# Value tiles of their own, third-chunk operands over finished gate sums, and S5 rows kept as loaded, in one layer of a streaming encoder on one Trainium2 core

## The chip, the cores and the metric

The kernel runs on one core of a Trainium2 chip. The metric is the device time of one execution in microseconds (us), as the median of several runs. An engine is named as in the profile: PE (TensorE matrix passes) and PEld (its weight loads), DVE (VectorE), ACT (ScalarE), POOL (GpSimd) and SP (SyncE, which in this kernel issues the loads and stores). Each engine works through its own instructions in order; semaphores tie the engines together.

## The reference

The reference computes one step of an encoder layer for two groups of requests with shared weights: one prompt of 1024 tokens and 8 decode requests of 16 tokens. The kernel treats them as 1152 tokens of width 1024.

```
h = rmsnorm(x, g_pre1);  z = h @ w_in
u_ssm, u_pool, q_mem = z[:, :512], z[:, 512:768], z[:, 768:]
y_ssm = gelu(s5_scan(u_ssm))
y_ssm = y_ssm * sigmoid(y_ssm @ w_glu + b_glu)
y_pool = multiscale_pool(u_pool);  y_mem = attention(q_mem, mem_k, mem_v)   # decode: cached k, v
gates = sigmoid(h @ w_gate + b_gate)            # 3 x 1024 columns
merged = gates_0 * (y_ssm @ w_br_ssm) + gates_1 * (y_pool @ w_br_pool) + gates_2 * (y_mem @ w_br_mem)
x += rmsnorm(merged @ w_out, g_post1)
x += rmsnorm(conv_ffn(rmsnorm(x, g_pre2)), g_post2)
```

All data are float32, and the outputs include the new states.

## The kernel before

**Precision and passes.** A matrix product in the kernel is three passes over operands that are split in two. `split` (L60 to L63) makes the split of a tile: ACT copies a rounded high part (L62), DVE subtracts it from the tile (L63, the low part). `mm3` (L100 to L106) issues high by high (L102), high by low (L105) and low by high (L106). Names that end in hi and lo are such pairs; a weight is loaded into a tile `rawt` (`load_raw`, L67) and split into `whi` and `wlo`.

**Tokens.** The 1152 tokens lie in three chunks of 384. A matrix pass is 128 x 384, and a result tile of 128 x 384 takes one bank of PSUM. There are two groups of four banks, called pc and ps in the profile.

**Order.** One scheduler goes through the whole program and lists the instructions of each engine in the order in which they seem ready to it; calls like `high_priority`, `keep_in_program_order` and `issue_after` steer it. A tile taken from a pool waits until the last use of the buffer that it gets. Nearly all loads and stores are issued by SP, in order, so a load that waits for its buffer holds up all loads and stores behind it.

**Stages that matter here.**

- *Phase 1.* Projection, S5 scan, pooling branch and attention. Attention of the decode requests (`attention_decode`, L719) is interleaved with that of the prompt. For its second half, four value tiles `cv` of 512 KB are loaded (L765), each for two requests, and multiplied with the transposed probabilities `PT` (L768, 16 small matrix instructions a tile). All four take tag "U", a pool of two buffers. The prompt's attention issues L847 to L850 (scores), L851 (exponential on ACT), L854 (values), L855 and L856 (division on DVE).
- *Gates in phase 1.* Interleaved with this, gate columns 8 to 15 for all chunks, then (L925 on) the gates that are needed for chunk 2, odd ones first. Their sigmoids are kept in memory (`Dsg`).
- *`blocks`* (L953). The remaining 16 gate columns of chunks 0 and 1 are computed by Strassen's method. For this, x of chunks 0 and 1 is loaded again (tiles `xT`, L164, behind the last `cv` load by `issue_after`), scaled by the norm (L962) and combined into operand blocks B11, B21 and others, tiles `bB` and `bT`, each split into a high and a low part. The first products with B11 and B21 stand in the gate loop of phase 1: the product with B11 is copied into a tile `u` (L942), eight of which (tag "su") live until phase S.
- *Phase S* (`phase_s`, L986). For eight pairs of gate columns j, five block products each, which are added to `u` (L1054 to L1062, partly on POOL), passed through a sigmoid (L1047) and stored in `Dsg` (L1048). At pair 6 the operands of the branches for chunks 0 and 1 are loaded (`load_pair`, L1091: attention results from `Dmem`, pooling results from `Dpool`) and split into `ohi` and `olo`.
- *Phase G* (`phase_g`, L1139). Branch weights `w_bmp` are loaded, then the operands of chunk 2 (the call of `operands`, the line behind the first `load_w`). For each column tile f and chunk c the two branches MEM and POOL are multiplied, weighted by the gate tiles `sgl` (L1085) and added to `merged`. Then GLU (`glu`, L1115) for each chunk: `load_ssm` loads the S5 output rows (L1101) into `br` tiles and splits them; the product with `w_glu` goes through a sigmoid on ACT (L1122); POOL adds the two halves of the S5 row together again as `ys` (L1124); DVE multiplies (L1125); and the result is split for the last branch (`w_brs`).

The next stages (phase O and the feed-forward network) stay as they are. The rows `rb` hold the norm's factors of a chunk, spread over the partitions.

Of the kernel before, what the change touches and what calls it, by code (L numbers as in the profile page):

```python
# [7 lines left out]
F32 = mybir.dt.float32  # L8
# [23 lines left out]
class K:  # L32
# [685 lines left out]
    def attention_decode(self, P):  # L718

        nc = self.nc  # L720
        cq = P.tile([128, 768], F32, tag="CA", name="cq")
        Qbd = cq[:, 0:512].rearrange("p (h b e s) -> p h b e s", h=2, b=8, e=2)
        nc.gpsimd.memset(cq[:, 0:512], 0.0)
        qdt = cq[:, 512:768].rearrange("p (h j k) -> p h j k", h=2, j=8)
        for hp in range(2):
            nc.sync.dma_start(qdt[:, hp], self.Dq[hp].rearrange("p (j k) -> p j k", j=8)[:, :, 128:144])
        for hp in range(2):
            qd = qdt[:, hp].rearrange("p j (b k) -> p b j k", k=2)
            for e in range(2):
                es = slice(64 * e, 64 * e + 64)  # L730
                nc.gpsimd.tensor_copy(Qbd[es, hp, :, e, :].rearrange("p b (j k) -> p b j k", k=2), qd[es])
        sc = [self.sm().rearrange("p (h m) -> p h m", h=2) for _ in range(2)]
        for b in range(8):
            if b % 2 == 0:
                ck = P.tile([128, 2, 2, 256], F32, tag="U", name="ck")
                nc.sync.dma_start(ck, self.I["ck"][b // 2])
            r = 32 * (b % 4)
            for hp in range(2):
                nc.tensor.matmul(sc[b // 4][r:r + 32, hp, :], Qbd[:, hp, b].rearrange("p e s -> p (e s)"),
                                 ck[:, b % 2, hp, :], start=True, stop=True, tile_position=(0, r))  # L740
        yield
        mx = P.tile([128, 4], F32, tag="mxd", name="mx")
        for e in range(2):
            nc.vector.tensor_reduce(mx[:, 2 * e:2 * e + 2], sc[e], axis=AX.X, op=OP.max)
        nc.vector.tensor_scalar(mx, mx, -0.125, None, op0=OP.mult)
        rs = P.tile([128, 4], F32, tag="rsum", name="rsum")
        p = P.tile([128, 4, 256], F32, tag="bc", name="pd")
        for h in range(4):
            nc.scalar.activation(p[:, h, :], sc[h // 2][:, h % 2, :], AF.Exp, bias=mx[:, h:h + 1], scale=0.125,
                                 accum_out=rs[:, h:h + 1])  # L750
        nc.vector.reciprocal(rs, rs)
        nc.vector.tensor_mul(p, p, rs[:, :, None].to_broadcast([128, 4, 256]))
        PT = P.tile([128, 4, 2, 128], F32, tag="V", name="PT")
        for a in range(2):
            t = self.sm().rearrange("p (h m l) -> p h m l", h=2, m=2)
            for h in range(2):
                for m in range(2):
                    nc.tensor.transpose(t[:, h, m, :], p[:, 2 * a + h, m * 128:(m + 1) * 128], self.ident)
            nc.vector.tensor_copy(PT[:, 2 * a:2 * a + 2], t)
        yield  # L760
        od = self.sm().rearrange("p (b h s) -> p b h s", b=8, h=2)
        for b in range(8):
            if b % 2 == 0:
                cv = P.tile([128, 2, 2, 256], F32, tag="U", name="cv")
                self.att_half = nc.sync.dma_start(cv, self.I["cv"][b // 2])  # L765
            for hp in range(2):
                for m in range(2):
                    nc.tensor.matmul(od[:, b, hp, :], cv[:, b % 2, m, hp * 128:hp * 128 + 128],  # L768
                                     PT[:, 2 * (b // 4) + hp, m, 32 * (b % 4):32 * (b % 4) + 32], start=m == 0, stop=m == 1)
        ot = P.tile([128, 2, 8, 16], F32, tag="tmp", name="otd")  # L770
        for hp in range(2):
            for e in range(2):
                es = slice(64 * e, 64 * e + 64)
                nc.vector.tensor_copy(ot[es, hp].rearrange("p j (b k) -> p b j k", k=2),
                                      od[es, :, hp, 16 * e:16 * e + 16].rearrange("p b (j k) -> p b j k", k=2))
        for hp in range(2):
            nc.sync.dma_start(self.Dmem[hp].rearrange("p (j k) -> p j k", j=8)[:, :, 128:144], ot[:, hp])
        yield
# [84 lines left out]
    def phase1(self):  # L863
        nc, tc = self.nc, self.tc
# [7 lines left out]
        self.Dsg = D.tile([24, 3, 128, 384], F32, name="Dsg")  # L872
        self.rbs = ExitStack()
        self.rb = self.rbs.enter_context(tc.tile_pool(name="rb", bufs=1)).tile([128, 3, 384], F32, name="rb")
        su = self.rbs.enter_context(tc.tile_pool(name="su", bufs=8))
        with ExitStack() as ctx:
            def pool(name, bufs):
                return ctx.enter_context(tc.tile_pool(name=name, bufs=bufs))
# [55 lines left out]
            self.su = []  # L934
            for m in self.strassen_gates()[0::2]:
                gw = gates(m, (2,))
                self.su.append(su.tile([128, 384], F32, tag="su", name="u"))
                for n, ks in (("B11", slice(0, 4)), ("B21", slice(4, 8))):
                    b = self.block(self.pc(), [w[:, ks] for w in gw], n)
                    with tc.high_priority():  # L940
                        if n == "B11":
                            nc.scalar.activation(self.su[-1], b, AF.Copy)  # L942
                        else:
                            sg = P.tile([128, 384], F32, tag="sg", name="sg")
                            nc.vector.tensor_add(sg, self.su[-1], b)
                            nc.scalar.activation(sg, sg, AF.Sigmoid, bias=self.vec[:, V_BGATE + m:V_BGATE + m + 1])
                            nc.sync.dma_start(self.Dsg[m, 0], sg)
# [44 lines left out]
    def phase_s(self):  # L992
        nc, tc = self.nc, self.tc
        V, G = nc.vector, nc.gpsimd
        with ExitStack() as ctx:
            def pool(name, bufs):
# [4 lines left out]
            P = self.P = _Multi(None, {n: self.gs.enter_context(tc.tile_pool(name="g" + n, bufs=b, side="right",  # L1001
                                                                             reuse_waits="tile"))
                                       for n, b in (("pl", 5), ("opa", 16))})
            self.om, self.op = [], []

            def operands(c, tag):
# [62 lines left out]
            for j in range(8):  # L1069
                cur, nxt = nxt, weights(j + 1) if j < 7 else None  # L1070
                if j == 6:
                    for c in range(2):
                        operands(c, "opa")
                for p in (6, 5, 7, 3, 4):
                    prod(cur, p)

# [16 lines left out]

    def load_ssm(self, P, c):

        op = []
        for q in range(0, 4, 2):
            r = self.rawtile([128, 2, 384], "br")
            for j, n, k0, k1, col in self.pieces(c):
                for i in range(n):  # L1100
                    self.nc.sync.dma_start(r[:, :, col + 144 * i:col + 144 * i + k1 - k0],  # L1101
                                           self.DY[q:q + 2, 7 - j - i, :, :, k0:k1].rearrange("q c g k -> (c g) q k"))
            op += [self.split_op(P, r[:, i], "opb") for i in range(2)]
        return op

    def split_op(self, P, r, tag):
        t = [P.tile([128, 384], F32R, tag=tag, name=n) for n in ("ohi", "olo")]
# [6 lines left out]

    def glu(self, P, w, c):  # L1115
        nc = self.nc
        y = self.load_ssm(P, c)
        out = []
        for o in range(4):
            b = self.proj(w[o // 2], c, 4, lambda kt, c: y[kt][0], lambda kt, c: y[kt][1], wk=4 * (o % 2))  # L1120
            sg = P.tile([128, 384], F32, tag="sg", name="sg")
            nc.scalar.activation(sg, b, AF.Sigmoid, bias=self.vec[:, V_BGLU + o:V_BGLU + o + 1])  # L1122
            ys = P.tile([128, 384], F32, tag="pl", name="ys")
            nc.gpsimd.tensor_add(ys, y[o][0].bitcast(F32), y[o][1].bitcast(F32))  # L1124
            nc.vector.tensor_mul(sg, ys, sg)  # L1125
            out.append(self.split_op(P, sg, "opa" if c < 2 else "opb"))
        return out

    def branch(self, P, bw, nk, wk, g, f, c, x):
# [9 lines left out]
    def phase_g(self):  # L1139
        nc, tc = self.nc, self.tc  # L1140
        with ExitStack() as ctx:
            def pool(name, bufs):
                return ctx.enter_context(tc.tile_pool(name=name, bufs=bufs, side="right", reuse_waits="tile"))
            P = self.P
            P.by.update({"opb": pool("gopb", 22), "sg": pool("gsg", 4)})
            bw = self.load_w(self.I["w_bmp"][0])
            self.operands(2, "opb")
            om, op = self.opx(self.om), self.opx(self.op)
            self.merged = [self.mtile([128, 8, 384], F32, f"mg{c}") for c in range(3)]
            for f in range(8):  # L1150
# [682 lines left out]
def emit(tc, I, O, dbg=None, stop=99):  # L1833
    with ExitStack() as ctx:
        k = K(tc, ctx, I, O, dbg)
        k.consts()
        k.phase1()
        if stop < 2:
            return
        k.phase_s()  # L1840
        k.rbs.close()
        k.phase_g()
        k.gs.close()
        k.dump("merged", k.merged[0])
        if stop < 3:
            return
        with tc.tile_pool(name="w2", bufs=4, reuse_waits="tile") as w2:
            k.w2 = w2
            k.phase_o()
            k.phase_u()  # L1850
            k.phase_d()
# [142 lines left out]
```

## Time and profile before

| | us |
|---|---|
| median of 3 runs | 1559.93 (1559.21 to 1562.07) |
| profiled execution | 1558.77 |
| its span in the trace | 1556.9 |
| PE busy in the span | 1525.9 (98%) |
| DVE busy | 1105.2 (71%) |
| ACT busy | 625.0 (40%) |
| POOL busy | 457.3 (29%) |

Times in the trace count from the span's start. The span is that of the one core's instructions; the execution takes 1.87 us more. "Busy" leaves out instructions that only issue a transfer or wait. Since matrix passes overlap, a pass shows about 0.34 us though a new one starts every 0.17 us. A row of the timeline gives the start, the duration, the engine, the line and the tiles, and in brackets how long the engine had been idle and which instruction of another engine ended the wait. The granted clock of TensorE was 0.99 on average over the execution.

### The profile page before, as it was taken

To read this page: it belongs to the slowest core of one execution; us is meant where nothing else is said; L and a number is where in the kernel's file an instruction comes from. 1 tells how busy PE (TensorE), PEld (TensorE's weight loads), DVE (VectorE), ACT (ScalarE), POOL (GpSimd) and SP (SyncE) were. 2 spreads that over 40 slices of the span, in tenths; PEclk is the share of its full clock that TensorE was granted. 3 is DMA by queue.
4 is the path that set the end of the run, shared out by engine and by line. 5 is a ranking of instruction groups with operands and counts; after the bars stand their busy time and mean duration, and the time that the engine had idled before them with its cause. 6 is when DMAs were issued, how large, how long until landed. Compare 5 with 4: busy or idle time off the path is not lost.

```text
span 1556.9 us, 23095 instructions
## 1 busy us (share of the span) xinstructions
PE 1525.9 (98%) x8914; PEld 1490.7 (96%) x8914; DVE 1105.2 (71%) x1714; ACT 625.0 (40%) x958; POOL 457.3 (29%) x441
## 2 busy tenths in 40 slices
PE   9999999998999899999999999999999999999997
PEld 7999998878899899999999999999999999999997
DVE  7956987659788668627687665665565569888876
ACT  8313445443555324435454333333333343233322
POOL 0000010000011345500025444344344311565545
PEclk9999999998999999999999999999999999999998
DMA  7533334554254674512413222212212133222224
GB/s 269 170 102 109 104 114 165 182 159 149 75 176 160 217 204 134 160 46 99 155 41 130 82 77 85 72 56 85 72 67 75 71 120 131 75 102 97 92 72 167
DMA packets 109262, 183.51 MB, mean 118 GB/s; under 512 B 24416, under 2 KB 76768, under 8 KB 109152
## 3 DMA queue, kind: packets, MB, share of 16 engines
q1 hardware_dynamic: 108576, 181.54, 35.4%
q8 instruction: 70, 1.15, 0.3%
q10 hardware_dynamic: 576, 0.49, 0.1%
q14 instruction: 40, 0.33, 0.1%
HBM read 134.27 MB, written 47.73 MB: 117 GB/s over the span
## 4 chain that ended last, share of the span: by engine, by line
PE 84%; DVE 7%; DMA 4%; ACT 3%; issue 2%; POOL 0%; DVEq 0%; ACTq 0%; SPq 0%; POOLq 0%
PE pc L102 14%; PE pc L106 14%; PE pc L105 14%; PE ps L102 12%; PE ps L105 12%; PE ps L106 12%; DMA Ts<-DG 1%; PE ps L854 1%; DMA rawt<-in_w_bmp 1%; DMA DG<-gs 1%; ACT hhi L125 1%; DVE mg L1264 1%; ACT whi L62 0%; DVE wlo L63 0%; DVE olo L63 0%
## 5 line engine op out<-in xcount | busy, mean ns | idle before, releaser
L102 PE MATMUL pc<-hhi,whi 128*128 128x384 f32 x504 | 171.1, 340 | 0.0
L105 PE MATMUL pc<-hlo,whi 128*128 128x384 f32 x504 | 170.8, 339 | 0.3 <-DVE hlo L126 0.3
L106 PE MATMUL pc<-hhi,wlo 128*128 128x384 f32 x504 | 169.8, 337 | 0.6 <-DVE wlo L63 0.6
L63 DVE TENSOR_TENSOR wlo<-rawt,whi 128x1024 fp32r<-128x1024 f32 (+1 forms) x99 | 123.0, 1243 | 58.5 <-ACT whi L62 58.1
L62 ACT ACTIVATE whi<-rawt 128x1024 fp32r<-128x1024 f32 (+1 forms) x99 | 103.4, 1045 | 146.7 <-PE pc L105 78.2
L62 ACT ACTIVATE S<-S 128x512 fp32r<-128x512 f32 x112 | 70.0, 629 | 161.4 <-PE ps L106 87.9
L63 DVE TENSOR_TENSOR S<-S,S 128x512 fp32r<-128x512 f32 x112 | 91.1, 818 | 50.0 <-ACT S L62 47.9
L106 PE MATMUL pc<-h2hi,wlo 128*128 128x384 f32 x352 | 118.9, 338 | 0.0
L105 PE MATMUL pc<-h2lo,whi 128*128 128x384 f32 x352 | 118.3, 336 | 0.5 <-DVE h2lo L63 0.5
L102 PE MATMUL pc<-h2hi,whi 128*128 128x384 f32 x352 | 118.3, 336 | 0.0
L102 PE MATMUL ps<-bT,S 128*128 128x384 f32 x304 | 101.5, 334 | 0.0
L105 PE MATMUL ps<-bT,S 128*128 128x384 f32 x304 | 101.5, 334 | 0.0
L106 PE MATMUL ps<-bT,S 128*128 128x384 f32 x304 | 101.5, 334 | 0.0
L105 PEld LDWEIGHTS pc<-hlo,whi 128*128 128x128 f32 x504 | 94.7, 188 | 3.1 <-DVE hlo L126 1.1
L106 PEld LDWEIGHTS pc<-hhi,wlo 128*128 128x128 f32 x504 | 94.6, 188 | 2.4 <-DVE wlo L63 1.2
L102 PEld LDWEIGHTS pc<-hhi,whi 128*128 128x128 f32 x504 | 94.7, 188 | 1.7 <-issue 0.4
L62 ACT ACTIVATE dhi<-dwr 128x1024 fp32r<-128x1024 f32 x38 | 39.6, 1058 | 83.9 <-PE pc L105 49.4
L102 PE MATMUL ps<-ohi,whi 128*128 128x384 f32 x192 | 65.2, 342 | 2.4 <-ACT ohi L62 2.4
L199 DVE TENSOR_TENSOR sg<-pc,rb 128x384 f32<-128x384 f32 x63 | 34.6, 553 | 46.1 <-PE pc L106 40.2
L105 PE MATMUL ps<-olo,whi 128*128 128x384 f32 x192 | 65.4, 341 | 1.9 <-DVE olo L63 1.9
L105 PEld LDWEIGHTS pc<-h2lo,whi 128*128 128x128 f32 x352 | 66.0, 187 | 0.8 <-DVE h2lo L63 0.8
L85 POOL TENSOR_TENSOR rs_y<-rs_v,mhalf 128x3 f32<-128x3 f32 (+1 forms) x13 | 14.0, 1080 | 177.3 <-ACT rs_v L83 177.3
(487 smaller groups left out, 4653.7 us busy)
## 6 DMA issues: line engine op xcount, KB each, us to landing
rawt<-in_w_up SPq DMA_DIRECT2D x44, 512.0 KB, 3.3
rawt<-in_w_gate SPq DMA_DIRECT2D x40, 512.0 KB, 3.8
Dsg<-sg SPq DMA_DIRECT2D x72, 192.0 KB, 1.8
sgl<-Dsg SPq DMA_DIRECT2D x72, 192.0 KB, 2.9
Dact<-t SPq DMA_DIRECT2D x22, 576.0 KB, 3.6
dwr<-in_w_down SPq DMA_DIRECT2D x22, 512.0 KB, 3.5
xT<-in_xT SPq DMA_DIRECT2D x20, 384.0 KB, 7.0
dBr<-Dact SPq DMA_DIRECT2D x8, 768.0 KB, 5.1
```

The lines of the kernel that those rows point to most:

```text
L62: a = nc.scalar.activation(hi, src, AF.Copy)
L63: return a, (eng or nc.vector).tensor_sub(lo, src, hi)
L85: nc.gpsimd.tensor_tensor(y, v, self.mhalf[:, 0:n], op=OP.pow)
L102: i = nc.tensor.matmul(out, whi, xhi, start=start, stop=False)
L105: nc.tensor.matmul(out, whi, xlo, start=False, stop=False)
L106: nc.tensor.matmul(out, wlo, xhi, start=False, stop=stop)
L125: a = nc.scalar.activation(hi[:, k, :], x[:, k, :], AF.Copy, scale=g)
L199: self.nc.vector.tensor_mul(sg, b, self.rb[:, c, :])
L854: nc.tensor.matmul(o, va[:, m, 2 * hp + e, :], pT[:, m, :], start=m == 0, stop=m == 1)
L1264: V.scalar_tensor_tensor(oT[:, f, :], oT[:, f, :], self.vec[:, V_GPRE2 + f:V_GPRE2 + f + 1], rb, op0=OP.mult, op1=OP.mult)
```

## The change

The change has three parts.

1. The four `cv` tiles get buffers of different tags: the first two stay with "U", the third takes tag "bc" and the fourth "Xs", which are buffers of earlier work in phase 1.
2. The branch operands of chunk 2 are loaded at pair 7 of phase S, and not at the start of phase G. Their split tiles take buffers of tag "su", in which the sums `u` of the gate pairs lay. So that eight of them are there, the sums of pairs 6 and 7 move into the rows `rb[:, 0]` and `rb[:, 1]`. The pool of "su" is closed after phase G, and the pool "opb" has 14 buffers instead of 22. The split GLU output of chunk 2 also lies in "su".
3. The S5 rows are loaded into one tile `y` of 128 x 4 x 384 for each chunk, and not into `br` tiles. GLU's product on DVE reads the loaded row itself, so that the twelve additions on POOL are gone.

```diff
-                cv = P.tile([128, 2, 2, 256], F32, tag="U", name="cv")
+                cv = P.tile([128, 2, 2, 256], F32, tag=("U", "U", "bc", "Xs")[b // 2], name="cv")
...
-        su = self.rbs.enter_context(tc.tile_pool(name="su", bufs=8))
+        su = self.sup = self.rbs.enter_context(tc.tile_pool(name="su", bufs=8, reuse_waits="tile"))
...
-                self.su.append(su.tile([128, 384], F32, tag="su", name="u"))
+                j = len(self.su)
+                self.su.append(su.tile([128, 384], F32, tag="su", name="u") if j < 6 else self.rb[:, j - 6, :])
...
+            P.by["su"] = self.sup
...
+                if j == 7:
+                    operands(2, "su")
...
-        op = []
+        op, raw = [], self.mtile([128, 4, 384], F32, "y")
...
-            r = self.rawtile([128, 2, 384], "br")
+            r = raw[:, q:q + 2]
...
-        return op
+        return op, raw
...
-        y = self.load_ssm(P, c)
+        y, raw = self.load_ssm(P, c)
...
-            ys = P.tile([128, 384], F32, tag="pl", name="ys")
-            nc.gpsimd.tensor_add(ys, y[o][0].bitcast(F32), y[o][1].bitcast(F32))
-            nc.vector.tensor_mul(sg, ys, sg)
-            out.append(self.split_op(P, sg, "opa" if c < 2 else "opb"))
+            nc.vector.tensor_mul(sg, raw[:, o], sg)
+            out.append(self.split_op(P, sg, "opa" if c < 2 else "su"))
...
-            P.by.update({"opb": pool("gopb", 22), "sg": pool("gsg", 4)})
+            P.by.update({"opb": pool("gopb", 14), "sg": pool("gsg", 4)})
...
-            self.operands(2, "opb")
...
         k.phase_s()
-        k.rbs.close()
         k.phase_g()
         k.gs.close()
+        k.rbs.close()
```

The scheduler lists some instructions in another order now. Line numbers behind the change are one to four higher than before.

The SP queue around the value loads. Before, the third and fourth `cv` load, and then those of x again (L164), stand behind the stores of the gates and of the pooling and attention results:

```order
L67 DMA rawt<-in_w_gate 128x1024
L857 DMA Dmem<-yt 128x4x128
L765 DMA cv<-in_cv 128x1024
L925 DMA Dsg<-sg 128x384
L765 DMA cv<-in_cv 128x1024
L164 DMA xT<-in_xT 128x768 x4
L653 DMA E<-Dz_91 128x8x128
```

and now, from the first `cv` load on:

```order
L765 DMA cv<-in_cv 128x1024
L925 DMA Dsg<-sg 128x384
L67 DMA rawt<-in_w_gate 128x1024
L765 DMA cv<-in_cv 128x1024 x2
L164 DMA xT<-in_xT 128x768 x2
L67 DMA rawt<-in_w_gate 128x1024
L925 DMA Dsg<-sg 128x384
L164 DMA xT<-in_xT 128x768 x2
L925 DMA Dsg<-sg 128x384
L67 DMA rawt<-in_w_gate 128x1024
L765 DMA cv<-in_cv 128x1024
```

The four value loads and the first half of x moved to where the first two value loads stood.

The PE order there, with `cv` (L768) and the first products with B11 (`bB_3481`). Before:

```order
L854 MATMUL ps<-at_2255 128x512
L768 MATMUL ps<-PT,cv 128x32 x8
L854 MATMUL ps<-at_2255 128x512
L768 MATMUL ps<-PT,cv 128x32 x24
L102 MATMUL pc<-bB_3481,whi 128x384
L105 MATMUL pc<-bB_3481,whi 128x384
```

and now (the products with B11 have moved ahead of the last L854 of the first half, and the value products all stand in one place behind them):

```order
L854 MATMUL ps<-at_2255 128x512
L105 MATMUL pc<-hlo,whi 128x384
L106 MATMUL pc<-hhi,wlo 128x384
L102 MATMUL pc<-bB_3481,whi 128x384
L105 MATMUL pc<-bB_3481,whi 128x384
L854 MATMUL ps<-at_2255 128x512
L847 MATMUL ps<-at_2253 128x512
```

The SP queue at the end of phase S, with the loads of branch operands (`br`) and branch weights (`w_bmp`). Before:

```order
L1091 DMA br<-Dmem 128x2x384
L1091 DMA br<-Dpool 128x2x384
L67 DMA rawt<-in_w_bmp 128x1024
L1048 DMA Dsg<-sg 128x384
L1091 DMA br<-Dmem 128x2x384
L1048 DMA Dsg<-sg 128x384
L1091 DMA br<-Dpool 128x2x384
L1048 DMA Dsg<-sg 128x384
L67 DMA rawt<-in_w_bmp 128x1024 x2
```

and now:

```order
L1095 DMA br<-Dmem 128x2x384
L1095 DMA br<-Dpool 128x2x384
L1095 DMA br<-Dmem 128x2x384
L1050 DMA Dsg<-sg 128x384
L1095 DMA br<-Dpool 128x2x384
L1050 DMA Dsg<-sg 128x384 x2
L67 DMA rawt<-in_w_bmp 128x1024 x4
```

The first branch weight moved behind the operands of chunk 2 and three gate stores, and the four weights now stand together.

## The prediction

> **What bounds the kernel now.** I read first the page's busy times, then what TensorE waited for, then tables by stage with the clock.
>
> ```profile
> span 1556.9 us, 23095 instructions
> PE 1525.9 (98%) x8914; PEld 1490.7 (96%) x8914; DVE 1105.2 (71%) x1714; ACT 625.0 (40%) x958; POOL 457.3 (29%) x441
> ...
> PE pc L102 <- ACT bB L62: 4.0, 1, 4.0
> PE ps L102 <- ACT ohi L62: 2.4, 1, 2.4
> PE ps L768 <- DMA cv<-in_cv: 2.0, 2, 1.1
> PE pc L102 <- ACT sg L1122: 1.9, 2, 1.5
> PE ps L105 <- DVE olo L63: 1.9, 1, 1.9
> PE pc L105 <- DVE bB L63: 1.6, 1, 1.6
> ...
> 346.00:358.00 12.00, 6.39 (x23) 5.86 (x24) 9.37 (x17) 2.97 (x2) 0.74 (x2) 0.50 1.02 324
> 524.00:528.00 4.00, 0.46 (x2) 0.20 (x2) 3.26 (x6) 2.87 (x6) 1.49 (x2) 0.75 0.55 172
> 528.00:532.00 4.00, 4.00 (x13) 4.00 (x14) 2.55 (x4) 0.00 (x0) 0.79 (x1) 0.50 0.91 298
> 597.00:603.00 6.00, 4.12 (x22) 3.48 (x22) 5.58 (x7) 2.45 (x6) 3.35 (x3) 1.00 0.14 55
> ```
>
> The second row is TensorE's, busy for 1525.9 of 1556.9 us: 31.0 us idle in all. The next six are its longest waits (total, times, longest). In the window rows (length, busy time of PE, PEld, DVE, ACT, POOL, granted clock, DMA share, GB/s) three stages stand out, and in two of them the clock falls to 0.50, so that they cost more than the idle time shows. The change touches exactly these three.
>
> **Stage 1, decode values to block operands.** Timeline rows (start, duration, engine, line, idle before and its releaser):
>
> ```profile
> 332.28 1.02 PE L854 MATMUL ps<-at 128*128 128x512 f32 x2
> ...
> 340.23 1.87 PE L768 MATMUL ps<-PT,cv 128*128 128x32 f32 x16
> 342.13 0.33 SPq L765 DMA_DIRECT2D cv<-in_cv  x1
> 342.51 2.01 SPq L164 DMA_DIRECT2D xT<-in_xT  x4
> 347.14 1.15 DVE L962 SCALAR_TENSOR_TENSOR xT<-xT,vec,rb 128x384 f32<-128x384 f32 x2 [2.62 <-DMA xT<-in_xT]
> 352.11 1.48 ACT L62 ACTIVATE bB<-xT 128x1536 fp32r<-128x1536 f32 x1 [12.62 <-DVE xT L962]
> 354.11 1.75 DVE L63 TENSOR_TENSOR bB<-xT,bB 128x1536 fp32r<-128x1536 f32 x1
> 359.24 0.33 PE L102 MATMUL pc<-bB,whi 128*128 128x384 f32 x1
> 360.45 0.33 PE L102 MATMUL pc<-hhi,whi 128*128 128x384 f32 x1
> ```
>
> The fourth cv load is issued at 342.13, after the second batch of L768 freed its buffer, and the xT loads stand behind it; so scaling (L962), the copy of B11 (ACT) and its remainder (DVE) all end after TensorE wants them. From 359.24 to 360.45 seven passes go by: 0.173 us a pass at full clock. A batch of 16 L768 takes 1.87 us. Without the wait the second batch ends at 342.1, two more take 3.74, and the 13th pass of B11 and B21 comes 12 x 0.173 = 2.1 later: 347.9. It came at 359.24. **Loss 11.3 us**, part wait and part half clock.
>
> **The change there.** The third and fourth value tiles no longer wait for a buffer. All four cv loads and the eight xT loads go out from about 302 on, where the first two cv loads stood. That crowds the loads and the in-order engines earlier, so it is priced:
>
> ```profile
> 300.00:320.00 20.00, 20.00 (x110) 17.48 (x109) 12.20 (x17) 11.88 (x17) 0.23 (x2) 1.00 0.70 231
> 305.00:310.00 5.00, 5.00 (x32) 4.58 (x32) 3.79 (x6) 2.47 (x5) 0.00 (x0) 1.00 0.99 345
> 310.00:325.00 15.00, 15.00 (x73) 12.79 (x72) 7.06 (x6) 11.13 (x14) 0.11 (x1) 1.00 0.53 169
> ...
> xT<-in_xT SPq DMA_DIRECT2D x8, 384.0 KB, 7.0
> cv<-in_cv SPq DMA_DIRECT2D x4, 512.0 KB, 3.8
> ```
>
> From 300 to 320 the kernel moved 20 x 231 = 4.6 MB. Two cv and eight xT add 2 x 0.52 + 8 x 0.39 = 4.2 MB. At the 345 GB/s of the full window the 8.8 MB take 25 us: all has landed by 325, and the four xT of B11 earlier, about 313 (three cv, two weights, four xT and the gate stores stand ahead: 4.6 MB from 300). Then eight L962 at 0.57, 1.48 on ACT and 1.75 on DVE make 7.8 us: B11 at about 321, B21 by 325 to 333. In the new order TensorE reaches B11 three passes after the place where the L854 of 332.28 stood, about 334. VectorE was busy 7.06 of 15 us there, so 4.6 for L962 and 3.5 for two remainders fit; with the third and fourth product it is nearly full until the L855 reciprocals are done. I take the whole loss less 0.5 us: a gain of 10.8, bounds 4 (B21 late, one clock drop) and 11.3.
>
> **Stage 2, start of the branches.**
>
> ```profile
> 505.75 0.34 SPq L67 DMA_DIRECT2D rawt<-in_w_bmp  x1
> 509.54 0.37 SPq L1091 DMA_DIRECT2D br<-Dmem  x1
> 512.69 7.58 SPq L67 DMA_DIRECT2D rawt<-in_w_bmp  x2
> 518.68 1.22 DVE L63 TENSOR_TENSOR wlo<-rawt,whi 128x1024 fp32r<-128x1024 f32 x1 [4.91 <-ACT whi L62]
> 519.01 0.33 PE L102 MATMUL ps<-ohi,whi 128*128 128x384 f32 x1
> 522.99 0.34 PE L106 MATMUL ps<-ohi,wlo 128*128 128x384 f32 x1
> 523.65 1.06 ACT L62 ACTIVATE whi<-rawt 128x1024 fp32r<-128x1024 f32 x1 [1.71 <-DMA rawt<-in_w_bmp]
> 525.12 1.75 ACT L62 ACTIVATE ohi<-br 128x384 fp32r<-128x384 f32 x4
> 533.26 0.34 PE L106 MATMUL ps<-ohi,wlo 128*128 128x384 f32 x1
> ...
> rawt<-in_w_bmp SPq DMA_DIRECT2D x4, 512.0 KB, 4.1
> ```
>
> Chunk 2's rows are asked for at 509.54, yet their copies (525.12) stand on ACT behind a weight that came in at 523.65. TensorE stops twice (the 2.4 and 1.9 of the list above), then runs at half clock. The pass at 533.26 is the 19th after 522.99; at 0.173 it would come at 526.28. **Loss 7.0 us.** The change puts chunk 2's loads and copies ahead of all branch weights; I place the copies near 514, 9 us before their use. What is late next is the first branch weight. Its load was issued at 505.75 and now comes behind the chunk-2 loads and three gate stores, with the other three: about 512.7. With 4.1 to landing, 1.06 and 1.22 it is ready at 519.1, and TensorE wants it from 519.0 to 519.4. I take 0.5 us of wait, bounds 0 and 3 (a loading time like that of the xT, 7.0). Gain 6.5, bounds 1 and 7.0: 1 where the wait also drops the clock.
>
> The clock fell in 524 to 528, with 0.46 us of work in 4 us, and stayed at 1.00 in 597 to 603, where the waits were 1.9 us in sum. [...]
>
> **Stage 3, GLU.**
>
> ```profile
> L1124 POOL TENSOR_TENSOR ys<-ohi,olo 128x384 f32<-128x384 f32 x12 | 14.9, 1255 | 4.6 <-DVE sg L1125 4.5
> ...
> 599.13 1.37 DVE L1125 TENSOR_TENSOR sg<-ys,sg 128x384 f32<-128x384 f32 x1
> 601.58 0.45 PE L102 MATMUL pc<-ohi,whi 128*128 128x384 f32 x1 [1.50 <-ACT sg L1122]
> 602.16 0.54 DVE L1125 TENSOR_TENSOR sg<-ys,sg 128x384 f32<-128x384 f32 x1
> ```
>
> The twelve additions on POOL (1.26 us each) go; the product on VectorE reads the loaded row. Beside POOL it took 1.37, alone 0.54. The chain from sigmoid to the next free bank shortens by up to 1.26 + 0.8 = 2 us a step, more than the longest wait of 1.5. Gain 1.9, bounds 0 and 1.9. The row loads are now issued earlier, among the gate loads of the branches; the windows quoted above show DMA shares of 0.91 (528 to 532) and 0.14 (597 to 603), room enough on average, so I put nothing on it.
>
> **Sum.** 10.8 + 6.5 + 1.9 = 19.2. Some small waits must open while TensorE runs 11 us ahead of its weights and gates: between 360 and 520 no wait of TensorE is listed, so there is slack, but how much the trace doesn't say; I take 1.5 (0 to 6). Net 17.7. The profiled execution took 1558.77 us, 1.87 more than its span; 1558.77 - 17.7 = 1541.1. The runs' median lies 1.16 above that execution; I split the difference and say **1541.5**.
>
> **The rivals.**
> (a) *The first branch weight replaces chunk 2 as the late one.* A wait of 3 us instead of 0.5 and the clock at half as in 528 to 532: 2.5 more of wait and some 3 of clock, **1547**. For it: its margin is nil. Against: PE already has 0.4 us between its first pass and the first that needs the remainder.
> (b) *VectorE becomes the bound in stage 1.* Its queue is in order; L962 waiting for xT (2.62 in the row above) now stands ahead of reciprocals and gate evacuations. One late reciprocal holds TensorE some 3 us, and at half clock for some 8 us it loses 4 more: **1549**. For it: VectorE nearly full after 320. Against: B11 has 13 us to spare.
> (c) *The gain is given back.* With TensorE 11 us ahead, the block products of the next 160 us find weights or gates late by as much, and the branch start as well: about **1558**, no change. Against it: no TensorE wait there now.
> (d) *Slower.* The crowded loads hold VectorE at L962 so long that TensorE runs out of free banks in stage 1. Place: 305 to 334. Four banks of 24 passes at 0.173 are 16.6 us of cover; to cost more than the 17.7 gained TensorE must stand about 12 us and then lose 6 at half clock, so VectorE must be held over 28 us. The loads take 25 us at full rate, all of it before 325. Price at 33 us of hold: 16 standing and 6 at half clock, **1564**.
>
> **How the numbers follow.** Forecast 0.62; (a) 0.12, (b) 0.14, (c) 0.06, (d) 0.06. This kernel's measurement tells 0.2% (3 us) from no change. (a), (b) and the forecast are all faster: 0.87 with a little of the forecast's edge given away, 0.86; the same 0.07; slower 0.07. The forecast alone spans 1537.5 (nothing opens, all gained: 1558.77 - 20.2 = 1538.6, less a run's scatter) to 1546. The range reaches over (a) and (b): 1536 to 1553.
>
> **What would show it.** In the profile after: cv issued four times before 315 and no wait of TensorE on cv or bB; the clock at 1.00 in what was 346 to 358. No wait on ohi or olo at the start of the branches; if one is left, it should name whi or wlo of the first branch weight. No wait on the sigmoid. TensorE's idle time near 14 to 17 us. The prediction is wrong if TensorE waits in stage 1 for L855 or exponentials, if the clock drops again near 510 or 520, or if the block products show waits on weights that are not there now.

## The result, and the profile after

The change makes the kernel faster: median 1546.17 us (1543.30 to 1548.72 over four runs) against 1560.89 (1559.21 to 1562.07), a ratio of 0.9906 with a 95% interval of 0.9883 to 0.9929. That is 14.7 us where 17.7 were forecast from the profiled execution; the forecast of 1541.5 was 4.7 us too low, and the time lies inside the range of 1536 to 1553. The profiled execution of the changed kernel took 1548.72, the slowest of its four runs. Two of the runs behind this document, one of 1658.34 us ("spread, first weight ahead") and one of the kernel before beside it (5340.35), fell in a slower state and are left out of medians and ratios.

The span and the busy times of the changed kernel, from the page:

```profile
span 1546.9 us, 23088 instructions
PE 1524.9 (99%) x8914; PEld 1489.2 (96%) x8914; DVE 1097.8 (71%) x1714; ACT 627.4 (41%) x960; POOL 451.4 (29%) x429
```

TensorE's longest waits in it (total, times, longest):

```profile
PE ps L102 <- DVE sgl L1158: 2.7, 3, 2.1
PE ps L267 <- DVE pr L394: 1.4, 1, 1.4
PE ps L634 <- DVE Xs L603: 1.3, 1, 1.3
PE ps L95 <- ACT diag L93: 1.2, 1, 1.2
PE ps L102 <- DVE mg L1136: 1.1, 2, 0.9
...
PE ps L106 <- DVE wlo L63: 0.5, 1, 0.5
```

All six waits of the list before are gone: those on `cv`, on `bB`, on chunk 2's `ohi` and `olo`, and on the sigmoid. TensorE's idle time fell from 31.0 to 22.0 us. New are the waits on L1158 and L1136 (VectorE's products of a branch with its gate tile, which free a PSUM bank), and half a microsecond on the first branch weight, as forecast. Windows of the changed kernel (length, busy time of PE, PEld, DVE, ACT, POOL, granted clock, DMA share, GB/s):

```profile
344.00:352.00 8.00, 8.00 (x61) 7.51 (x60) 7.91 (x8) 3.58 (x5) 1.18 (x4) 1.00 0.57 182
352.00:358.00 6.00, 6.00 (x27) 6.00 (x27) 5.82 (x9) 0.00 (x0) 0.31 (x2) 0.50 0.65 202
510.00:528.00 18.00, 16.07 (x87) 14.70 (x87) 11.93 (x18) 5.77 (x9) 8.13 (x7) 1.00 0.82 266
528.00:532.00 4.00, 1.91 (x12) 1.59 (x11) 1.22 (x3) 1.77 (x3) 0.56 (x2) 1.00 0.77 214
532.00:536.00 4.00, 3.83 (x14) 3.38 (x15) 4.00 (x6) 1.05 (x3) 2.83 (x2) 0.61 0.35 93
```

The second row is the surprise: TensorE is busy for all of 352 to 358, waits for nothing that the profile lists, and still has half its clock. The last three rows are the start of the branches, where 1.9 and 2.1 us of idle time and a second fall of the clock are left.

Three marks in the trace divide the program by work that is the same in all kernels: the first block product with a `bT` operand, the first branch product, and the end of the span. Of the kernel before and of the change:

```profile
435.81 0.33 PE L102 MATMUL pc<-bT,S 128*128 128x384 f32 x1
```

```profile
427.65 0.33 PE L102 MATMUL pc<-bT,S 128*128 128x384 f32 x1
```

The table gives the first mark, the stretch to the second and the stretch from there to the end, of each kernel's profiled execution, with the median and the ratio from the timed runs. The kernels from the third row on are the experiments below. Each ratio is to runs of the kernel before on the same chip; their medians lay between 1559.4 and 1560.9, so medians of different rows compare only within some 1.5 us. The intervals of the ratios are wider than most differences between rows.

| kernel | to first `bT` | to first branch product | to the end | median | ratio (interval) |
|---|---|---|---|---|---|
| before | 435.8 | 83.2 | 1037.9 | | |
| the change | 427.7 | 83.2 | 1036.0 | 1546.2 | 0.9906 (0.9883 to 0.9929) |
| the change again | 429.3 | 83.2 | 1032.5 | 1545.9 | 0.9909 (0.9894 to 0.9925) |
| value tiles only | 428.7 | 83.2 | 1037.9 | 1551.1 | 0.9944 (0.9929 to 0.9959) |
| operands only | 436.4 | 83.2 | 1037.9 | 1557.0 | 0.9984 (0.9974 to 0.9993) |
| rows only | 436.2 | 83.2 | 1036.0 | 1558.5 | 0.9993 (0.9984 to 1.0003) |
| without rows | 427.3 | 83.2 | 1034.2 | 1548.3 | 0.9927 (0.9912 to 0.9942) |
| rows later | 427.3 | 83.2 | 1032.9 | 1544.7 | 0.9899 (0.9883 to 0.9916) |
| products spread | 424.2 | 83.2 | 1031.7 | 1542.2 | 0.9884 (0.9869 to 0.9899) |
| products twice | 442.3 | 83.2 | 1032.7 | 1560.8 | 1.0006 (0.9997 to 1.0015) |
| rows later and products spread | 424.1 | 83.2 | 1031.5 | 1541.0 | 0.9875 (0.9859 to 0.9892) |
| spread, first weight ahead | 424.1 | 83.2 | 1031.8 | 1541.0 | 0.9884 (0.9866 to 0.9901) |
| all three | 424.1 | 83.2 | 1033.2 | 1541.1 | 0.9879 (0.9861 to 0.9897) |

The middle stretch is the same to 0.01 us everywhere, so nothing is won or given back in the block products. In its profile the change won 8.2 us ahead of them and 1.9 behind. The last stretch is a coarse measure: from the 481st matrix pass behind the second mark to the end, where no kernel differs from another, the profiles lie between 944.0 us (rows later and products spread) and 945.8 (rows later).

### The profile page after: what moved, and what is told of

Same layout as the page of the kernel before. It is cut to its first block, busy times and chain, and to the rows that moved or that the text cites. A ratio compares the mean times of both kernels' runs of the same rounds, so it can differ in the third digit from the quotient of the medians.

```text
span 1546.9 us, 23088 instructions
## 1 busy us (share of the span) xinstructions
PE 1524.9 (99%) x8914; PEld 1489.2 (96%) x8914; DVE 1097.8 (71%) x1714; ACT 627.4 (41%) x960; POOL 451.4 (29%) x429
## 4 chain that ended last, share of the span: by engine, by line
PE 83%; DVE 7%; DMA 4%; ACT 3%; issue 2%; POOL 0%; DVEq 0%; ACTq 0%; SPq 0%; POOLq 0%
PE pc L106 14%; PE pc L102 14%; PE pc L105 14%; PE ps L102 11%; PE ps L105 11%; PE ps L106 11%; DMA Ts<-DG 1%; PE ps L854 1%; DMA DG<-gs 1%; ACT hhi L125 1%; DVE dB L63 1%; PE ps L768 1%; DVE mg L1265 1%; PE ps L1212 0%; PE ps L820 0%
## 5 line engine op out<-in xcount | busy, mean ns | idle before, releaser
L106 PEld LDWEIGHTS pc<-h2hi,wlo 128*128 128x128 f32 x352 | 66.2, 188 | 0.0
L102 PEld LDWEIGHTS pc<-h2hi,whi 128*128 128x128 f32 x352 | 66.1, 188 | 0.0
```

Source lines behind the costliest of these rows:

```text
L102: i = nc.tensor.matmul(out, whi, xhi, start=start, stop=False)
L106: nc.tensor.matmul(out, wlo, xhi, start=False, stop=stop)
```

## The experiments

### The parts alone

Each of the first three kernels is the one before with one part of the change; the fourth is the change without its third part.

```diff
 # value tiles only
-                cv = P.tile([128, 2, 2, 256], F32, tag="U", name="cv")
+                cv = P.tile([128, 2, 2, 256], F32, tag=("U", "U", "bc", "Xs")[b // 2], name="cv")
 # operands only: the lines on su, rb and operands(2, "su") of the change
 # rows only
-            ys = P.tile([128, 384], F32, tag="pl", name="ys")
-            nc.gpsimd.tensor_add(ys, y[o][0].bitcast(F32), y[o][1].bitcast(F32))
-            nc.vector.tensor_mul(sg, ys, sg)
+            nc.vector.tensor_mul(sg, raw[:, o], sg)
```

> The kernel before with part 1 alone (the four value tiles in buffers of their own). Theory: stage 1 loses its 11.3 us, but the value products, 64 of them now in one run of about 9 us, drop the clock once and give about 3 back, as in the profile after. So about 8.3 us less than before, 1552.5; clock 0.50 for some 6 us in or behind the run of L768, with no wait of TensorE there. Rival (the clock drop of the profile after is left over from something that parts 2 and 3 moved): no drop, 11 us less, about 1549.5. The stages at 520 and 597 keep their waits of 4.3 and 1.9 us.

Measured: 8.3 us less than the kernel before on the same chip (1551.07 against 1559.41), as the theory had it; its sum is right, but the fall was longer than the 6 us that it named. The granted clock was 0.80 from 350 to 351, 0.50 from there to 360 and 0.58 from 360 to 361, which is half clock for 10.2 us. The run of value products in this kernel's timeline (start, duration, engine, line):

```profile
346.36 9.83 PE L768 MATMUL ps<-PT,cv 128*128 128x32 f32 x64
```

and one window from inside it:

```profile
352.00:353.00 1.00, 1.00 (x6) 1.00 (x6) 0.97 (x1) 0.00 (x0) 0.00 (x0) 0.50 1.03 312
```

The clock falls without parts 2 and 3 too, in a run of 64 small instructions that none of TensorE's waits interrupts.

> The kernel before with part 2 alone (third-chunk operands at pair 7, over u). Theory: stage 2's loss of 7.0 goes but for the first weight's wait of about 0.5, and the gate tiles are not late, since the S5 rows are still loaded through the three shared tiles: 5 to 6.5 us less than before, 1554.5 to 1556. Rival (the six branch and GLU weights, now loaded in one run ahead of the gate tiles, make these late): waits on L1158 or L1136 of some 3 us and a clock drop as in the profile after, 0 to 2 us less than before, about 1559.5.

Measured: 2.4 us less, 1557.03. Neither forecast is right. The start of the branches did become nearly free of waits, but the stage behind it got worse, at least in this profile, which is of the slowest of the ten runs (1559.29). Windows of this kernel, first the branches, then GLU:

```profile
523.63:541.63 18.00, 17.62 (x100) 16.99 (x99) 9.72 (x18) 1.68 (x2) 8.97 (x8) 1.00 0.73 230
589.63:595.63 6.00, 3.84 (x19) 3.20 (x19) 5.88 (x7) 2.58 (x6) 3.16 (x3) 0.97 0.29 100
595.63:601.63 6.00, 5.80 (x18) 5.80 (x19) 5.09 (x9) 3.52 (x7) 1.19 (x1) 0.50 0.48 152
```

TensorE's waits in GLU:

```profile
PE pc L102 <- ACT ohi L62: 1.2, 1, 1.2
PE pc L105 <- DVE olo L63: 1.1, 1, 1.1
PE pc L102 <- ACT sg L1126: 0.9, 1, 0.9
```

GLU's three waits make 3.2 us where they were 1.9, and 2.2 us of idle time in one window of 6 us are followed by half clock. The branches end earlier, VectorE is nearly full (5.88 of 6 busy, with products that need an addition on POOL first), and TensorE meets that lag instead of the one it was relieved of. How often the ten runs had this fall, one profile doesn't say.

> The kernel before with part 3 alone (S5 rows kept as loaded, no additions on POOL). Theory: the two waits for the sigmoid (1.9 us) go, but the row loads come early among the gate loads and hold VectorE and ACT at the start of the branches: another 1 to 4 us of wait there on L1157 or L1134, so 1559 to 1563. Rival (early row loads are harmless): 1.9 less than before, 1559, and no new wait in 533 to 560.

Measured: 0.9 us less, 1558.48, with an interval that holds no change. The sigmoid waits are gone, and of the forecast new waits only one of 0.3 us on a gate product is listed. While TensorE still stood still for chunk 2's operands (waits of 1.9 and 1.9), the early row loads made nearly no wait of their own, so the rival fits this kernel better; the times can't tell its 1.9 us from 0.9.

> The changed kernel without part 3 (parts 1 and 2). Theory: the waits on L1158 and L1136 at 516 to 532 of the profile after come from the S5 rows that are loaded and split early, so they are gone here; the sigmoid waits of 1.9 us come back: 8.3 from stage 1 and 5 to 6.5 from stage 2 gained, 1546 to 1548, no slower than the changed kernel. Rival (weights in one run make the gate tiles late): waits on L1158 and L1136 stay at 3 to 4 us, and the time is 1.9 over the changed kernel, about 1549 to 1551.

Measured: 1548.34, 11.1 us less than before; the edge between both forecasts in time. Windows of this kernel at the branches and at GLU:

```profile
510.00:522.00 12.00, 10.94 (x60) 9.99 (x60) 8.66 (x12) 3.97 (x6) 5.87 (x5) 1.00 0.79 268
522.00:574.00 52.00, 52.00 (x301) 52.00 (x300) 34.63 (x58) 11.22 (x20) 28.16 (x27) 1.00 0.66 191
574.00:588.00 14.00, 10.71 (x59) 9.76 (x58) 13.88 (x16) 5.75 (x11) 9.55 (x8) 1.00 0.37 126
```

The waits on the gate products go down from 3.8 to 1.1 us and none is left after 522, as the theory wanted; GLU then loses 3.3 us, as with part 2 alone. Alone the parts give 8.3, 2.4 and 0.9, 11.6 in sum, and together 14.7; the interval of that last number runs from 11 to 18, so the times don't show that the parts are worth more together. The profiles show what part 3 does beside part 2: it takes GLU's lag away and brings waits to the start of the branches.

### The row loads at the start of the branches

In the profile of the change, the longest wait of TensorE at the start of the branches ends like this:

```profile
530.23 0.52 ACT L62 ACTIVATE ohi<-y 128x384 fp32r<-128x384 f32 x1 [3.98 <-DMA y<-DY]
530.66 1.04 ACT L62 ACTIVATE whi<-rawt 128x1024 fp32r<-128x1024 f32 x1
530.78 0.56 DVE L63 TENSOR_TENSOR olo<-y,ohi 128x384 fp32r<-128x384 f32 x1 [2.96 <-ACT ohi L62]
531.26 0.55 DVE L1158 TENSOR_TENSOR sgl<-ps,sgl 128x384 f32<-128x384 f32 x1
531.87 0.45 PE L102 MATMUL ps<-ohi,whi 128*128 128x384 f32 x1 [2.09 <-DVE sgl L1158]
```

ACT waits 3.98 us for an S5 row that is still on its way; VectorE waits 2.96 us for ACT with the remainder of that row; and the product L1158, which frees a bank, is behind it in VectorE's order. To test whether the rows are the cause, the row loads were held behind gate tiles of the branches:

```diff
+                    with self.tc.issue_after(self.gl[8 + (3, 5, 6)[c], 2].ins):
                         self.nc.sync.dma_start(r[:, :, col + 144 * i:...
```

> The changed kernel, with the loads of the S5 rows kept behind gate tiles of the branches (chunk 0's behind column tile 3, chunk 1's behind 5, chunk 2's behind 6). Theory: the waits on L1158 and L1136 in 514 to 533 of the profile after (3.8 us, and 1.9 of half clock) come from the row loads and splits that stand among the first gate tiles; with the rows later they go down to about 1, as in the run without part 3, without the sigmoid waits of that run: from the first branch product to the first product of the next phase 127 to 128 us instead of 132.25, time 4 to 5 us under the changed kernel. Rival (the gate tiles are late because six weights are loaded in one run just ahead of them): the waits stay near 3 us, 0 to 1 us gained.

Measured: 1544.72, 1.4 us under the change's 1546.17 where 4 to 5 were forecast, and the intervals of the two ratios overlap. In the profile the stretch from the first branch product to the end is 3.1 us shorter than in the first profile of the change (1032.9 against 1036.0), and no clock fall is left there. But a row that is asked for later holds up what stands behind it too:

```profile
540.77 0.53 ACT L62 ACTIVATE ohi<-y 128x384 fp32r<-128x384 f32 x1 [14.62 <-DMA y<-DY]
```

The copy of a weight (`whi`) is next on ACT, and TensorE waits 0.7 us for it, a wait that the change didn't have. To know what the change does by itself it was run again, unaltered:

> The changed kernel once more, unaltered, on the chip of the next two: its runs lay 5.4 us apart (1543.3 to 1548.7), and the profile of it was that of the slowest. Theory: the fall of the clock in the run of L768 comes every time, but the waits at the start of the branches differ from run to run with the loads' landing; so this profile shows the same stage 1 (about 3.4 us over the version with spread products) and a start of the branches that is up to 3 us shorter. Rival (every run is like the profile): the same 132 us from the first branch product to the next phase, waits on L1158 and L1136 of 3 to 4 us.

Measured: 1545.86, ratio 0.9909. TensorE's waits at the start of the branches in this second profile of the changed kernel:

```profile
PE ps L102 <- DVE sgl L1158: 1.1, 2, 0.7
PE ps L102 <- DVE mg L1136: 1.0, 3, 0.6
```

and the rows that belong to the copy at 530.23 and the pass at 531.87 of the first:

```profile
528.77 0.53 ACT L62 ACTIVATE ohi<-y 128x384 fp32r<-128x384 f32 x1 [2.56 <-DMA y<-DY]
530.41 0.44 PE L102 MATMUL ps<-ohi,whi 128*128 128x384 f32 x1 [0.69 <-DVE sgl L1158]
```

For the branches the theory holds: the longest wait was 0.7 us, the clock stayed at 1.00, and the stretch took 1032.5 us, 3.5 less. The kernel is the same; the row's copy starts 1.46 us earlier, and TensorE waits 1.40 us less. For stage 1 it doesn't hold: this profile is there 5.1 us behind the version with spread products, not 3.4. So the waits on gate products make 3.8 us and a fall of the clock in one execution, and 2.1 us and no fall in another. Moving the row loads later is not shown to gain anything against this second profile (1032.9 against 1032.5).

The start of the branches and GLU can be told apart by counting matrix passes of 128 x 384 from the first branch product on. In each of the four kernels below, the first 300 contain all listed waits of TensorE at the start of the branches, and the next 180 all its waits in GLU. Windows over the first 300 (a window counts each pass that touches it, so one or two more), of the kernel before, the change, the second profile of it and the kernel without rows:

```profile
519.01:578.32 59.31, 55.10 (x301) 54.52 (x301) 36.19 (x62) 11.82 (x21) 24.95 (x23) 0.94 0.73 222
510.86:570.26 59.40, 55.21 (x301) 53.16 (x301) 39.77 (x63) 12.59 (x20) 27.07 (x23) 0.97 0.79 241
512.48:569.03 56.55, 54.21 (x302) 51.71 (x301) 37.59 (x62) 11.39 (x18) 27.01 (x23) 1.00 0.82 252
510.51:564.48 53.97, 52.91 (x302) 51.96 (x302) 34.92 (x59) 10.92 (x17) 25.40 (x23) 1.00 0.78 234
```

and over the next 180, of the kernel before, the change and the kernel without rows (the second profile of the change has 31.21 as well):

```profile
578.32:612.09 33.77, 31.89 (x181) 31.25 (x181) 29.78 (x38) 16.19 (x30) 18.64 (x16) 1.00 0.37 116
570.26:601.47 31.21, 31.21 (x182) 31.21 (x182) 23.02 (x38) 16.29 (x30) 7.52 (x6) 1.00 0.34 107
564.48:599.90 35.42, 32.13 (x182) 31.18 (x181) 31.87 (x41) 16.37 (x32) 20.50 (x18) 1.00 0.41 135
```

At the start of the branches the change won nothing in its first profile (59.40 against 59.31) and 2.8 us in the second; the kernel without part 3 won 5.3. In GLU it won 2.6 us in both, where the kernel without part 3 lost 1.7. With the rows later the first 300 passes take 55.90 us, still 1.9 more than without part 3.

### The run of value products

In the changed kernel the value products (L768) of all four tiles stand in one run, which starts at 346.95 and is followed by the next product at 355.88. In the next kernel they are issued in groups, as soon as parts of the prompt's attention are done:

```diff
+            if b in (1, 3, 5):
+                yield
...
                     nc.vector.tensor_mul(yf[es], o[es], yf[es])
+                    if g == 0 and (hp, e) != (1, 1):
+                        next(dec)
```

> The changed kernel, with the decode value products (L768) issued in five groups between the score and value products of the prompt, instead of 64 instructions in one run. Theory: the granted clock falls in the profile after because a run of 9 us of small products keeps the array little used though TensorE never waits; with dense products between the groups the clock stays at 1.00 from 330 to 365 and 3 us are gained in stage 1. Rival (the clock falls for another reason, such as the loads at 350 to 354): a fall of the clock of about 6 us somewhere in 330 to 365 all the same, no gain.

Measured: 1542.16, ratio 0.9884. Groups of L768 in this kernel's timeline:

```profile
320.91 1.42 PE L768 MATMUL ps<-PT,cv 128*128 128x32 f32 x12
323.18 2.98 PE L768 MATMUL ps<-PT,cv 128*128 128x32 f32 x26
327.86 2.09 PE L768 MATMUL ps<-PT,cv 128*128 128x32 f32 x18
```

and windows of it:

```profile
320.00:330.00 10.00, 10.00 (x71) 8.70 (x71) 9.97 (x13) 6.42 (x7) 1.66 (x4) 1.00 0.98 355
330.00:360.00 30.00, 30.00 (x155) 26.91 (x155) 29.60 (x30) 14.61 (x17) 1.05 (x3) 1.00 0.28 79
```

The clock stays at 1.00, and the first `bT` product comes at 424.2, 3.4 us ahead of the change's: 11.6 us ahead of the kernel before, against the 11.3 that the prediction had worked out as that stage's whole loss. The loads ran at 355 GB/s beside the groups without a fall, so nothing here speaks for the rival (loads). The next kernel doubles the run; the second pass writes the same result again:

```diff
-                for m in range(2):
+                for r, m in ((0, 0), (0, 1), (1, 0), (1, 1)):
```

> The changed kernel, with each pair of value products (L768) issued twice (the second writes the same result again): 128 small instructions in one run. Theory: the fall of the clock comes about 5 us into the run and lasts to some 3 us after its end, so the added 64 instructions all run at half clock, 0.17 us each: 11 us more than the changed kernel. Rival (the fall comes and goes for another reason, a fixed 6 us): 64 x 0.117 = 7.5 us more.

Measured: 1560.82, 14.7 us more than the change, so all the gain is gone. The run in this kernel's timeline:

```profile
346.37 23.96 PE L768 MATMUL ps<-PT,cv 128*128 128x32 f32 x128
```

and windows from inside it:

```profile
350.08:369.93 19.85, 19.85 (x96) 19.85 (x95) 4.54 (x4) 0.00 (x0) 0.90 (x5) 0.50 0.26 78
364.00:368.00 4.00, 4.00 (x20) 4.00 (x21) 0.00 (x0) 0.00 (x0) 0.00 (x0) 0.50 0.00 0
```

At half clock a small instruction starts every 0.213 us in this trace, where the forecast had 0.17, so the 64 more cost 13.6 us, not 11, and the fall came 1.3 us earlier in the run. From 364 to 368 no load is under way, and the clock stays down. Broken up, the run brings no fall, and twice as long, a longer one: what brings the clock down here is the run of small products itself. By which property of it, no run here tells: at full clock a product of 128 x 32 starts in it every 0.11 us, where one of 128 x 384 starts every 0.17. So far the "little used" of the expectation holds; that it is what lowers the clock was the author's estimate, and not shown.

### Both, and the first weight ahead

> Both of the last edits together: rows later and value products spread. Theory: the two gains add, 7 to 8 us under the changed kernel, 1537 to 1540 where the kernel before takes 1559 to 1561. Rival (only one of them works): 3 to 5 us.

Measured: 1541.04 us, ratio 0.9875 (0.9859 to 0.9892), against 1537 to 1540 by the theory. It is 5.1 us under the change; spread products alone are 4.0 under it. What the later rows add can't be told from nothing. The last edit loads the first branch weight ahead of chunk 2's operands again:

```diff
                 if j == 7:
+                    self.bw0 = self.load_w(self.I["w_bmp"][0])
                     operands(2, "su")
```

> The changed kernel with the value products spread and the first branch weight loaded ahead of the third-chunk operands, as in the kernel before. Theory: beside the 3.4 us of stage 1, the waits that the late weight makes (0.5 on its low part, 0.9 on L1136 behind two weight remainders on VectorE) go: 4 to 5 us under the changed kernel, 1 under the version with spread products alone. Rival (third-chunk rows are late then, or another weight's remainder is in the way): no gain over that version.

> The three edits together: products spread, first weight ahead, S5 rows later. Theory: waits between 505 and 545 below 1 us in sum, time 1537 to 1540 where the kernel before takes 1560. Rival (the rows later make the GLU's first products wait): no better than the one before it.

Measured: 1541.01 with the products spread and the weight ahead, 1541.14 with the rows later as well. Neither differs from spread products alone (1542.16) by more than 1.2 us, and the intervals of the ratios overlap. The waits on L1141 and its fellows remain in the kernel with the weight ahead:

```profile
PE ps L102 <- DVE mg L1141: 1.7, 3, 0.9
PE ps L102 <- DVE sgl L1163: 0.5, 1, 0.5
```

No wait on the first weight's low part is listed, but neither is one with spread products alone or in the second profile of the change, and 2.2 us on gate products stay. With the rows later as well they make 2.5 us, where below 1 was forecast, and the copy of a weight 0.6 more. Hence what holds the branch start in these kernels is not the late first weight alone. Which of the gate tiles, row splits and weight remainders on VectorE sets it there stays open; the waits are worth about 2 us.

## Why the prediction was right, and where it was off

**Which stages lose time and why: right.** All the waits that it named went away, and the loss it worked out for stage 1 (11.3 us) is what the kernel with spread products won there (11.6).

**Stage 1, 10.8 us forecast, 8.2 won (6.5 in the second profile).** The step that failed is "I take the whole loss less 0.5 us", with the clock at 1.00 in what was 346 to 358. The operands were ready as worked out, and VectorE, nearly full, made TensorE wait for nothing, so rival (b) didn't come. But the value products, which other products and the waits had cut into batches, became one run, and the clock fell in it. The spread kernel puts the price at 3.4 us against the first profile of the change and 5.1 against the second.

**Stage 2, 6.5 forecast; nothing won in the first profile, 2.8 us in the second** (by the first 300 passes). The late first weight cost 0.47 us in the first, as forecast (0.5), and no listed wait in the second. The term that was mis-sized is the row loads of part 3, "I put nothing on it": in the first profile they made the wait of 2.09 us that the fall of the clock followed, in the second a row that landed earlier made 0.69, and without part 3 the passes took 2.6 to 5.4 us less. The DMA shares quoted for it were averages of the kernel before; what counted was when a row landed and what stood behind its split in the order of ACT and VectorE. Holding the rows back didn't win all of it, so how much of the loss is the place of the loads and how much the work of part 3 itself stays open.

**Stage 3, 1.9 forecast, 2.6 won.** The sigmoid waits are gone in every kernel with part 3. Beside part 2 it is worth more there: without part 3 GLU's waits grow to 3.2 or 3.3 us as soon as part 2 is there. But what it wins in GLU it partly loses in stage 2.

**Sum.** Over the 480 passes of stages 2 and 3 the change won 2.5 us in the first profile and 5.3 in the second, where 8.4 were forecast. The 1.5 us put aside was for small waits between 360 and 520, where none opened; the losses came elsewhere, by the clock in stage 1 (3.4 to 5.1) and at the branches. That the time still came within the range is partly luck: the range is 17 us wide and was drawn to reach over rivals, and the time lies next to the 1547 of rival (a), which came by another cause than the late weight. Rivals (c) and (d) are excluded by the middle stretch of 83.2 us in all kernels and by the absence of any listed wait of TensorE in stage 1. Two small slips of the working change nothing: half of 1.16 added to 1541.07 gives 1541.65, and 0.62, 0.12 and 0.14 add to 0.88.

**The signs it named.** Four `cv` loads before 315 and no wait on `cv`, `bB`, chunk 2's operands or the sigmoid: these came. The clock at 1.00 in stage 1, only the first weight late at the branches, and an idle time of 14 to 17 us (22.0 measured) did not, and the clock fell again at the start of the branches, near the place that it named as a sign of being wrong. So the gains were foretold better than what the change would newly lose.

**A wait and the clock.** The wait of 2.09 us in stage 2, ended at 531.87, was followed by half clock in 532 to 536 (0.61 on average). That is one case, and no run varied such a wait by itself. The lower bound of 1 for the stage, meant for a wait that also drops the clock, was still too high for that profile, in which the stage won nothing.

## What to carry to other kernels

A wait that cuts a run of small matrix instructions into batches also spreads them; when it is removed, look at what the run does once it is in one piece, and put larger passes between its groups. Here the 64 products in one run had half clock for 6.8 us, and in groups none; that was worth 3.4 us. When a transfer is made free to start earlier, look not only at its queue but at the first instruction that reads it, on an engine that works in order: what stands behind that instruction is what comes late. Here ACT waited 3.98 us for such a row, and TensorE 2.09 us for what came behind it. And an engine's lag that was hidden behind a stall turns up when the stall goes, so that a part's gain beside the others is not the gain that it has alone: GLU's waits grew from 1.9 to 3.2 us when part 2 took the stall ahead of them away.

## What the runs showed of the hardware

TensorE's clock went to half without a wait of TensorE, in runs of 64 or 128 matrix instructions of 128 x 32 (one every 0.11 us at full clock), 3.7 to 5.8 us after their start in six profiles, and not in groups of at most 26 with larger instructions between, in four profiles. The length of each fall can be read from windows at its edges. Of the changed kernel, the second profile of it, and the kernel with products twice:

```profile
351.00:352.00 1.00, 1.00 (x11) 1.00 (x11) 1.00 (x1) 0.36 (x1) 0.00 (x0) 0.99 1.05 332
358.00:360.00 2.00, 2.00 (x11) 2.00 (x10) 1.97 (x3) 0.41 (x1) 0.11 (x1) 0.80 0.41 59
```

```profile
350.00:351.00 1.00, 1.00 (x10) 1.00 (x10) 0.97 (x3) 0.45 (x1) 0.11 (x1) 0.89 0.97 365
360.00:362.00 2.00, 2.00 (x10) 2.00 (x10) 1.93 (x4) 0.49 (x1) 0.11 (x1) 0.74 0.34 39
```

```profile
350.00:351.00 1.00, 1.00 (x8) 1.00 (x7) 1.00 (x1) 0.00 (x0) 0.59 (x3) 0.54 0.00 0
372.00:376.00 4.00, 4.00 (x20) 4.00 (x19) 3.93 (x5) 0.49 (x1) 0.11 (x1) 0.75 0.30 33
```

Between the edges the clock is 0.50. A window of 2 us with 0.80 was at half for 0.8 us, and so on: the falls last from 351.98 to 358.8, from 350.78 to 361.04 and from 350.08 to 374.0, that is 6.8, 10.3 and 23.9 us. Read in the same way, the fall is 10.2 us with value tiles only, 6.8 without rows (0.71 in 352 to 353, 0.88 in 359 to 360) and 6.8 with rows later (0.64 and 0.95 there). The fall at the branches of the change's first profile, with 0.95 in 532 to 533 and 0.85 in 536 to 537, lasts 3.4 us, the shortest of these; the others are 2, 3 and 7 times as long. Counted in pieces of 3.4 us, each costs about half its length, 1.7 us: two pieces are the 3.4 us that the spread kernel won against the first profile (3.1 and 3.0 against the other two with two pieces), three are the 5.1 against the second (4.4 against value tiles only). Seven pieces with 64 more instructions at 0.11 would make 12.0 + 7.0 = 19.0, where the first `bT` product came 18.1 later; a part of the difference is that these instructions start every 0.109 us at full clock and every 0.213 at half clock, a little under twice that. So the 1.6 us between the two profiles of the change in stage 1 are one piece more. Why the lengths are such multiples, no run here tells.
